# A two-layer encoder trunk: the MLP's up projection with two matmuls per weight tile instead of three, pinned transposes and a second priority level

## The chip, the cores and the metric

The kernel runs on one core of one Trainium2 chip. The metric is the device time of one execution in microseconds (us), taken as the median over runs. Five engines work side by side, each in the order of its own queue: TensorE (PE in the profile, with its weight loads as PEld), VectorE (DVE), ScalarE (ACT), GpSimd (POOL) and SyncE (SP), which issues most of the DMAs. They meet through semaphores only.

## The reference

Two layers over x of 256 tokens x 1024 channels, all in float32:

```python
for l in range(DEPTH):                                   # DEPTH = 2
    xn = rms_norm(x, norm_mix_g[l])
    x = x + mixer(xn, w_in[l], ...)                      # four branches, gates, w_out
    hn = rms_norm(x, norm_ffn_g[l])
    x = x + jnp.square(jax.nn.relu(hn @ w_ffn_up[l])) @ w_ffn_down[l]
return rms_norm(x, final_norm_g)

def mixer(xn, ...):
    h = xn @ w_in                                        # 1024 x 6176
    # split into glu, gq, gk, gv, gr, glr, aq, ak, av, pin, gate
    ys = jnp.stack([conv(..), gla(..), attention(..), pool(..)], axis=2)
    proj = jnp.einsum('btnc,ncd->btnd', ys, w_branch)    # 4 x (256 -> 1024)
    merged = jnp.sum(jax.nn.sigmoid(gate) * proj, axis=2)
    return merged @ w_out
```

The MLP is 1024 -> 4096 -> 1024. GLA is a chunked gated linear attention in both directions, attention is windowed, and the convolution has 31 taps.

## The kernel before

**Precision.** Every large product is made of float32r matmuls on split operands: a number is held as a high part (rounded to float32r) and a low part (the rest). A product is high x high + high x low + low x high, all summed in one PSUM region. `mm3` (lines 308 to 315) does that with the weights stationary and 256 tokens moving, `mm3t` (lines 317 to 324) with 128 tokens of x stationary and 512 weight columns moving.

**Weights.** `layer_loads` lists the weight pieces (128 partitions x 1024 numbers) in the order of their use. `fetch` (line 263) issues a piece's DMA on SP's queue into one of 3 raw buffers; `split_w` (line 271) makes the high part on ACT (line 278) and the low part on DVE (line 279), into 5 buffers of each kind. `piece` asks for a piece and lets `look_ahead` split four pieces ahead of it.

**Stages of a layer.** The gla, glu, qk, attention, pool and gate columns of w_in; the branches, with GLA and attention written as generators that the string `TURNS` (line 34) steps through in turn, one `next` per letter; the branch projections (`project`) and gates in the order `GATE_SEQ` (lines 40 to 46), where A, B, C, L stand for pool, attention, GLA and convolution; the transposes of the merged result (`turn_merged`); the output projection (`out_part`); the MLP (`up`, `down`) in 16 chunks of 256 hidden columns.

**The MLP.** `up(c)` makes one PSUM tile of a chunk: 8 row tiles k of 128 times 2 halves t of the 256 columns times `mm3`, 48 matmuls. Its eviction (lines 1150 to 1153) is a Relu on ACT, the square on DVE, the high part `hh` on ACT and the low part `hl` on DVE. `down(c)` is 24 matmuls of 512 columns into four accumulators that live for the whole MLP. The loop is up(2), down(1), up(3), down(2) and so on; on entry up(0) and up(1) are done in two halves of K, with `turn_x` between.

**Transposes.** x and the merged result lie with tokens on partitions for the sums and with channels on partitions for the matmuls. `turn` makes four 128 x 128 transposes on PE into one PSUM bank. `turn_x(xh, xl, h, g, behind)` turns the half h of x's channels and splits it (`split_x`, lines 427 to 434: high on ACT at line 430, low on DVE at line 431). `TokenStats.add` sums the squares of x for the norm (ACT, line 387); the norm's factor is applied at the end of the MLP, through `R2`.

**What sets the order.** The program is written with tiles; a planner orders each engine's queue by priority and by its own reckoning of when an instruction is ready, and puts in the semaphores. The priority is the place in the program; `urgent()` brings a block forward by 4000 places. `tc.issue_after(ins)` queues what a block writes for `ins`'s engine behind `ins` on that engine's queue, and adds no wait. PSUM has two pools of four banks, `ps_mm` (tag mm) and `ps_ax` (tag ax).

Of the kernel before, what the change touches and what calls it, by code (L numbers as in the profile page):

```python
# [33 lines left out]
TURNS = "agagagagggagggaggg"  # L34
# [138 lines left out]
def trunk_kernel(ctx: ExitStack, tc: tile.TileContext, x, w, prm, wup, poolw, cst, out, depth, dbg=None):  # L173
# [33 lines left out]

    def urgent():
        return tc.high_priority(offset=URGENT)

# [707 lines left out]
    for l in range(depth):  # L918
        if l == 0:
# [4 lines left out]
            for f in range(4):  # L924
# [3 lines left out]
                for t in (2 * f, 2 * f + 1):  # L928
                    split_x(xh, xl, t, xT[:, t, :], gain0)
# [122 lines left out]

        def project(n, h):
            first = n == BR_ORDER[0]
            wt = piece(l, ("br", n, h))
            for it in range(2):
# [5 lines left out]
                with urgent():  # L1062
# [6 lines left out]

        def turn_merged(h):  # L1070
            for f in (2 * h, 2 * h + 1):
                with urgent():
                    ps = turn(merged, f, mmt)
                    last_cast[:] = [S.copy(mh[:, 2 * f : 2 * f + 2, :], ps)]
                    V.tensor_tensor(
                        ml[:, 2 * f : 2 * f + 2, :], ps, mh[:, 2 * f : 2 * f + 2, :].bitcast(F32), ALU.subtract
                    )

        ENDS = {("gate", C, 1): ({1: conv},)}
        for what, n, h in GATE_SEQ:  # L1080
# [12 lines left out]
        fh = xs_p.tile([P, KD, T], F32R, tag="xs", name=nm("fh"))  # L1093
# [239 lines left out]
```

## Time and profile before

| | |
|---|---|
| median of 3 runs | 804.95 us (804.7 to 805.72) |
| the profiled execution, own time | 803.58 us |
| its span (first to last instruction of the program) | 801.6 us |
| PE busy | 782.3 us, 98%, 4810 matmuls |
| PEld busy (weight loads) | 687.9 us, 86%, 4810 loads |
| DVE busy | 558.4 us, 70%, 799 instructions |
| ACT busy | 473.5 us, 59%, 708 instructions |
| POOL busy | 10.6 us, 1% |
| read from HBM | 136.71 MB, 172 GB/s over the span |

The profile is of one execution. Matmuls are pipelined: the printed duration of one reaches past the start of the next, so what a matmul costs in a stream is the distance from its start to the next one's. The time in brackets behind an instruction is how long its engine stood idle before it, and the instruction that released it. A name such as mm or ax is a PSUM tile's tag, fh and fl are the high and low halves of x in the MLP, hi and lo those of the weights.

### The profile page before, as it was taken

To read this page: it belongs to the slowest core of one execution; us is meant where nothing else is said; L and a number is where in the kernel's file an instruction comes from. 1 tells how busy PE (TensorE), PEld (TensorE's weight loads), DVE (VectorE), ACT (ScalarE), POOL (GpSimd) and SP (SyncE) were. 2 spreads that over 40 slices of the span, in tenths; PEclk is the share of its full clock that TensorE was granted. 3 is DMA by queue.
4 is the path that set the end of the run, shared out by engine and by line. 5 is a ranking of instruction groups with operands and counts; after the bars stand their busy time and mean duration, and the time that the engine had idled before them with its cause. 6 is when DMAs were issued, how large, how long until landed. Compare 5 with 4: busy or idle time off the path is not lost.

```text
span 801.6 us, 12340 instructions
## 1 busy us (share of the span) xinstructions
PE 782.3 (98%) x4810; PEld 687.9 (86%) x4810; DVE 558.4 (70%) x799; ACT 473.5 (59%) x708; POOL 10.6 (1%) x22
## 2 busy tenths in 40 slices
PE   8999999999999999999999999999998999999996
PEld 8998887787798999999899987878788999999995
DVE  6789998887655555555577999878876655555553
ACT  6789795764654444444468787848545544444442
POOL 2000000000000000000000000000000000000000
PEclk9999999999999999999999999999999999999999
DMA  7755544465546555566455565435654565556631
GB/s 273 233 167 180 160 153 137 133 184 182 189 142 195 185 186 187 188 194 191 138 183 183 163 203 158 136 108 163 211 177 154 169 204 184 185 189 183 194 116 53
DMA packets 41130, 138.56 MB, mean 173 GB/s; under 512 B 4528, under 2 KB 7280, under 8 KB 41072
## 3 DMA queue, kind: packets, MB, share of 16 engines
q1 hardware_dynamic: 39616, 137.05, 54.0%
q10 hardware_dynamic: 1456, 0.73, 0.3%
q8 instruction: 37, 0.61, 0.3%
q14 instruction: 21, 0.17, 0.1%
HBM read 136.71 MB, written 1.05 MB: 172 GB/s over the span
## 4 chain that ended last, share of the span: by engine, by line
PE 91%; DVE 3%; DMA 3%; ACT 2%; issue 1%; ACTq 0%; DVEq 0%
PE mm L322 10%; PE mm L323 10%; PE mm L324 10%; PE mm L314 9%; PE mm L315 9%; PE mm L313 9%; PE ax L322 9%; PE ax L323 9%; PE ax L324 9%; DMA raw<-in_w_dram 2%; DVE lo L279 2%; ACT hi L278 1%; PE ax L657 1%; PE ax L836 1%; PE mm L1214 1%
## 5 line engine op out<-in xcount | busy, mean ns | idle before, releaser
L279 DVE TENSOR_TENSOR lo<-raw,hi 128x1024 fp32r<-128x1024 f32 (+2 forms) x260 | 313.9, 1208 | 202.4 <-ACT hi L278 193.0
L278 ACT CAST hi<-raw 128x1024 fp32r<-128x1024 f32 (+2 forms) x260 | 269.6, 1037 | 265.5 <-PE mm L314 113.9
L314 PE MATMUL mm<-fl,hi 128*128 128x256 f32 x512 | 144.6, 284 | 3.0 <-DVE fl L431 3.0
L313 PE MATMUL mm<-fh,hi 128*128 128x256 f32 x512 | 143.6, 283 | 1.4 <-ACT fh L430 1.4
L315 PE MATMUL mm<-fh,lo 128*128 128x256 f32 x512 | 144.2, 283 | 0.0
L322 PE MATMUL mm<-hi,xh 128*128 128x512 f32 (+1 forms) x320 | 122.6, 387 | 1.4 <-ACT xh L430 1.2
L323 PE MATMUL mm<-lo,xh 128*128 128x512 f32 (+1 forms) x320 | 122.5, 383 | 0.4 <-DVE lo L279 0.4
L324 PE MATMUL mm<-hi,xl 128*128 128x512 f32 (+1 forms) x320 | 121.1, 382 | 0.0
L314 PEld LDWEIGHTS mm<-fl,hi 128*128 128x128 f32 x512 | 98.0, 192 | 4.8 <-DVE fl L431 3.8
L313 PEld LDWEIGHTS mm<-fh,hi 128*128 128x128 f32 x512 | 97.5, 192 | 2.9 <-ACT fh L430 1.8
L322 PE MATMUL ax<-hi,hh 128*128 128x512 f32 x256 | 100.0, 390 | 0.0
L323 PE MATMUL ax<-lo,hh 128*128 128x512 f32 x256 | 100.0, 390 | 0.0
L315 PEld LDWEIGHTS mm<-fh,lo 128*128 128x128 f32 x512 | 98.0, 192 | 0.1
L324 PE MATMUL ax<-hi,hl 128*128 128x512 f32 x256 | 97.0, 389 | 0.0
L322 PEld LDWEIGHTS mm<-hi,xh 128*128 128x128 f32 x320 | 59.8, 188 | 14.1 <-ACT xh L430 1.5
L323 PEld LDWEIGHTS mm<-lo,xh 128*128 128x128 f32 x320 | 60.1, 188 | 12.4 <-issue 1.0
L324 PEld LDWEIGHTS mm<-hi,xl 128*128 128x128 f32 x320 | 60.0, 188 | 11.3 <-issue 0.2
L324 PEld LDWEIGHTS ax<-hi,hl 128*128 128x128 f32 x256 | 48.1, 188 | 10.2
L322 PEld LDWEIGHTS ax<-hi,hh 128*128 128x128 f32 x256 | 48.2, 188 | 9.2
L323 PEld LDWEIGHTS ax<-lo,hh 128*128 128x128 f32 x256 | 48.2, 188 | 9.0
L315 PE MATMUL mm<-xh,lo 128*128 128x256 f32 x160 | 45.4, 285 | 0.9 <-DVE lo L279 0.9
L314 PE MATMUL mm<-xl,hi 128*128 128x256 f32 x160 | 45.2, 283 | 0.0
(265 smaller groups left out, 1022.4 us busy)
## 6 DMA issues: line engine op xcount, KB each, us to landing
raw<-in_w_dram SPq DMA_DIRECT2D x252, 512.0 KB, 3.6
raw<-in_w_dram SPq DMA_DIRECT2D x6, 288.0 KB, 2.9
xT<-in_x_dram SPq DMA_DIRECT2D x4, 256.0 KB, 4.7
cst_t<-in_cst_dram SPq DMA_DIRECT2D x1, 608.0 KB, 5.6
out_dram<-yo SPq DMA_DIRECT2D x2, 256.0 KB, 2.4
out_dram<-yo ACTq DMA_DIRECT2D x2, 256.0 KB, 2.4
raw<-in_w_dram SPq DMA_DIRECT2D x1, 432.0 KB, 4.7
poolw_t<-in_poolw_dram SPq DMA_DIRECT2D x2, 128.0 KB, 4.3
```

Source lines behind the costliest of these rows:

```text
L278: a = S.copy(h[:, :n], r[:, :n])
L279: V.tensor_tensor(lo[:, :n], r[:, :n], h[:, :n].bitcast(F32), ALU.subtract)
L313: mm(o, a, xh[:, kx, :], start=start, stop=False, skip_group_check=True)
L314: mm(o, a, xl[:, kx, :], start=False, stop=False, skip_group_check=True)
L315: return mm(o, b, xh[:, kx, :], start=False, stop=stop, skip_group_check=True)
L322: mm(o, xh[:, kx, tk], wh[:, k, :], start=start, stop=False)
L323: mm(o, xh[:, kx, tk], wl[:, k, :], start=False, stop=False)
L324: return mm(o, xl[:, kx, tk], wh[:, k, :], start=False, stop=stop)
L657: mm(ot[:, h, :], pt[:, jt, h, it * P : (it + 1) * P], qkv[:, jt, 384 + 64 * g : 448 + 64 * g], start=jt == 0, stop=jt == 1,)
L836: mm(ps[32 * b : 32 * b + 32, jt], kk[:, j0 : j0 + 32], q[:, :, j0 : j0 + 32], start=True, stop=True, tile_position=(0, 32 * b),)
L1214: mm(ps[:, t, :], xt[:, it, c : c + P], dgs[it], start=True, stop=True)
```

## The change

Five things change together.

1. In `up`, the two halves of x lie side by side in a tile `fx` of [128, 4, 2, 256], so that one 512-column matmul takes a high weight tile to both: high x high lands in the first half of a PSUM bank, high x low in the second. The low weight tile meets the high half in a 256-column matmul onto the first half. Each of the two 128-column halves of a chunk now has a bank of its own, so a chunk holds two of the four banks of `ps_mm`. At eviction ACT copies the second half to SBUF, DVE adds it to the first, and the square takes the sum; the Relu on ACT is gone.
2. `turn_x` returns its last transpose, and the next group of matmuls (`out_part(3,1)`, `up(1)`'s first half, `down(15)` of the second half, the second `gvl`) is queued behind it. `turn_merged(0)` moves from behind ("br", C, 1) to behind the first half of ("br", L, 1).
3. A second level of priority, `critical()`, of 8000 places, is used for the transposes and splits of x, the merged transposes, the last branch's merging, the additions to x and part of the tail.
4. The sums of squares for the MLP's norm move from the end of the output projection to behind the first chunks of the MLP, at plain priority, and `st.inverse()` with them.
5. `TURNS` is shorter: GLA takes nine steps instead of twelve, so that its tail runs where `next(turns["g"], None)` stands behind ("br", B, 0), and attention's last two steps come earlier.

```diff
-TURNS = "agagagagggagggaggg"
+TURNS = "agagagaggagggag"
...
+    def after(t):
+
+        return tc.issue_after(t.ins) if t is not None else nullcontext()
+
     def urgent():
         return tc.high_priority(offset=URGENT)
+
+    def critical():
+        return tc.high_priority(offset=2 * URGENT)
 
     URGENT = 4000
...
-    def split_x(xh, xl, kt, src, g):
-
-        with urgent():
-            a = S.activation(xh[:, kt, :], src, AF.Copy, scale=g[:, kt : kt + 1])
-            V.scalar_tensor_tensor(
-                xl[:, kt, :], src, g[:, kt : kt + 1], xh[:, kt, :].bitcast(F32), ALU.mult, ALU.subtract
-            )
+    def split_x(xh, xl, src, gain):
+
+        with critical():
+            a = S.activation(xh, src, AF.Copy, scale=gain)
+            V.scalar_tensor_tensor(xl, src, gain, xh.bitcast(F32), ALU.mult, ALU.subtract)
         return a
...
-                nc.tensor.transpose(ps[:, t, it * P : (it + 1) * P], src[:, it, c : c + P], ident)
-        return ps
-
-    def turn_x(xh, xl, h, g, behind):
+                last = nc.tensor.transpose(ps[:, t, it * P : (it + 1) * P], src[:, it, c : c + P], ident)
+        return ps, last
+
+    def turn_x(parts, h, g, behind):
 
         with tc.issue_after(behind.ins):
-            turn_x_now(xh, xl, h, g)
-
-    def turn_x_now(xh, xl, h, g):
-        for f in (2 * h, 2 * h + 1):
-            with urgent():
-                ps = turn(xt, f, axt)
-            for t in range(2):
-                split_x(xh, xl, 2 * f + t, ps[:, t, :], g)
+            for f in (2 * h, 2 * h + 1):
+                with critical():
+                    ps, last = turn(xt, f, axt)
+                for t in range(2):
+                    kt = 2 * f + t
+                    split_x(*parts(kt), ps[:, t, :], g[:, kt : kt + 1])
+        return last
...
         for i, (k0, k1) in cuts if l == 0 else cuts[:2]:
-            done = gvl(i, k0, k1)
+            with after(turned if l and i == 1 else None):
+                done = gvl(i, k0, k1)
             if l and i == 0:
-                turn_x(xh, xl, 1, col(l, 0, 8), done)
+                turned = turn_x(x_parts, 1, col(l, 0, 8), done)
...
                 th = gates.pop((n, h, it))
-                with urgent():
+                if (n, h, it) == (L, 1, 0):
+                    with tc.issue_after(done.ins):
+                        turn_merged(0)
+                with critical() if n == L else urgent():
...
-            if (what, n, h) == ("br", C, 1):
-                with tc.issue_after(done.ins):
-                    turn_merged(0)
...
-        fh = xs_p.tile([P, KD, T], F32R, tag="xs", name=nm("fh"))
-        fl = xs_p.tile([P, KD, T], F32R, tag="xs", name=nm("fl"))
+
+        fx = [xs_p.tile([P, KD // 2, 2, T], F32R, tag="xs", name=nm("fx")) for _ in range(2)]
+
+        def f_parts(kt):
+            a = fx[kt // 4][:, kt % 4]
+            return a[:, 0, :], a[:, 1, :]
+
...
+        turned = None
         for h in range(2):
             for i in (2, 3):
-                done = out_part(i, h)
+                with after(turned if (i, h) == (3, 1) else None):
+                    done = out_part(i, h)
                 if (i, h) == (2, 1):
-                    turn_x(fh, fl, 0, col(l, 8, 8), done)
+                    turned = turn_x(f_parts, 0, col(l, 8, 8), done)
             for it in range(2):
                 xv = xt[:, it, 512 * h : 512 * h + 512]
-                with urgent():
+                with critical():
                     V.scalar_tensor_tensor(xv, acc[it, h], 0.5, xv, ALU.mult, ALU.add)
-            for it in range(2):
-                with urgent():
-                    st.add(it, h)
...
             if c not in ups:
-                ups[c] = mmt()
+                ups[c] = [mmt((P, 2, T)) for _ in range(2)]
             ps = ups[c]
             for i in parts:
-                wt = piece(l, (("up", c), i))
+                wh, wl = piece(l, (("up", c), i))
                 for k in range(4):
+                    f = fx[i][:, k]
                     for t in range(2):
-                        kk = 4 * i + k
-                        done = mm3(ps[:, t, :], wt, k, t * P, fx, kk, kk == 0 and t == 0, kk == 7)
+                        w1 = slice(t * P, (t + 1) * P)
+                        first, last = i + k == 0, (i, k) == (1, 3)
+                        mm(ps[t], wh[:, k, w1], f, start=first, stop=False, skip_group_check=True)
+                        done = mm(
+                            ps[t][:, 0, :], wl[:, k, w1], f[:, 0, :], start=False, stop=last, skip_group_check=True
+                        )
...
             r = gh_p.tile([P, 2, T], F32, tag="gh", name=nm("r"))
+            z = t2()
...
             with urgent():
-                S.activation(r, ps, AF.Relu)
-                V.scalar_tensor_tensor(r, ps, 0.0, r, ALU.max, ALU.mult)
+                for t in range(2):
+                    S.copy(z[:, t, :], ps[t][:, 1, :])
+                    V.tensor_tensor(r[:, t, :], ps[t][:, 0, :], z[:, t, :], ALU.add)
+                V.scalar_tensor_tensor(r, r, 0.0, r, ALU.max, ALU.mult)
                 S.copy(hh, r)
                 V.tensor_tensor(hl, r, hh.bitcast(F32), ALU.subtract)
...
             for c in range(2):
-                done = up(c, (i,))
+                with after(turned if (i, c) == (0, 1) else None):
+                    done = up(c, (i,))
                 if (i, c) == (0, 0):
-                    turn_x(fh, fl, 1, col(l, 8, 8), done)
-        with urgent():
-            R2 = st.inverse()
+                    turned = turn_x(f_parts, 1, col(l, 8, 8), done)
+        for h in range(2):
+            for it in range(2):
+                st.add(it, h)
+        R2 = st.inverse()
...
             for h in range(2):
                 for c in (14, 15):
-                    done = down(c, (0, 1), (h,))
+                    with after(turned if (c, h) == (15, 1) else None):
+                        done = down(c, (0, 1), (h,))
                     if (c, h) == (14, 1):
-                        turn_x(xh, xl, 0, col(nxt, 0, 8), done)
+                        turned = turn_x(x_parts, 0, col(nxt, 0, 8), done)
...
                     add_mlp(it, h)
-                    with urgent():
+                    with critical():
                         st.add(it, h)
```

## Rows read from the trace of the kernel before

**Rows 1.** The page: engines' busy time, PE's granted clock by slice.

```profile
PE 782.3 (98%) x4810; PEld 687.9 (86%) x4810; DVE 558.4 (70%) x799; ACT 473.5 (59%) x708; POOL 10.6 (1%) x22
...
PEclk9999999999999999999999999999999999999999
```

**Rows 2.** The page: the chain that ended last, by engine.

```profile
PE 91%; DVE 3%; DMA 3%; ACT 2%; issue 1%; ACTq 0%; DVEq 0%
```

**Rows 3.** Order of time, PE, one MLP chunk: start, duration, line, operands, count.

```profile
249.18 0.28 PE L315 MATMUL mm<-fh,lo 128*128 128x256 f32 x1
249.29 0.28 PE L313 MATMUL mm<-fh,hi 128*128 128x256 f32 x1
...
254.69 0.40 PE L322 MATMUL ax<-hi,hh 128*128 128x512 f32 x1
254.93 0.40 PE L323 MATMUL ax<-lo,hh 128*128 128x512 f32 x1
...
256.08 0.39 PE L322 MATMUL ax<-hi,hh 128*128 128x512 f32 x1
...
259.93 0.39 PE L324 MATMUL ax<-hi,hl 128*128 128x512 f32 x1
```

**Rows 4.** Groups by line and form: count | busy us, mean ns | idle.

```profile
L279 DVE TENSOR_TENSOR lo<-raw,hi 128x1024 fp32r<-128x1024 f32 x252 | 307.8, 1223 | 199.8 <-ACT hi L278 190.7 <-issue 8.6
...
L1151 DVE SCALAR_TENSOR_TENSOR r<-mm,r 128x512 f32<-128x512 f32 x32 | 21.9, 684 | 1.6 <-ACT r L1150 1.6
...
L1150 ACT ACTIVATE r<-mm 128x512 f32<-128x512 f32 x32 | 18.9, 592 | 1.9 <-PE mm L315 1.9
...
L431 DVE SCALAR_TENSOR_TENSOR fl<-ax,prm_t,fh 128x256 fp32r<-128x256 f32 x16 | 7.1, 475 | 0.0
L430 ACT ACTIVATE fh<-ax,prm_t 128x256 fp32r<-128x256 f32 x16 | 6.7, 468 | 0.0
```

**Rows 5.** Windows, steady MLP: PE, PEld, DVE, ACT, POOL busy, clock, DMA.

```profile
232.00:400.00 168.00, 168.00 (x1059) 152.74 (x1058) 93.48 (x95) 79.07 (x94) 0.00 (x0) 1.00 0.58 183
```

**Rows 6.** Order of time, DVE, that chunk's last step of the eviction.

```profile
259.87 0.68 DVE L1153 TENSOR_TENSOR hl<-r,hh 128x512 fp32r<-128x512 f32 x1
```

**Rows 7.** Order of time, PE and DVE, entry to the first MLP.

```profile
216.07 1.04 PE L442 MATMUL ax<-cst_t,xt 128*128 128x128 f32 x8
...
216.36 1.28 DVE L1122 SCALAR_TENSOR_TENSOR xt<-ax,xt 128x512 f32<-128x512 f32 x2
...
217.79 0.39 PE L313 MATMUL mm<-fh,hi 128*128 128x256 f32 x1 [0.68 <-ACT fh L430]
...
219.22 0.38 PE L314 MATMUL mm<-fl,hi 128*128 128x256 f32 x1 [0.93 <-DVE fl L431]
...
226.64 0.39 PE L314 MATMUL mm<-fl,hi 128*128 128x256 f32 x1 [0.54 <-DVE fl L431]
```

**Rows 8.** Order of time, PE, behind the first merged transposes.

```profile
189.82 0.50 PE L322 MATMUL mm<-hi,ysh 128*128 128x512 f32 x1 [0.55 <-DVE gate L1066]
```

**Rows 9.** Order of time, PE, the first matmul of the second layer.

```profile
402.51 0.40 PE L322 MATMUL mm<-hi,xh 128*128 128x288 f32 x1 [1.23 <-ACT xh L430]
```

**Rows 10.** Order of time, PE and ACT, the end of GLA.

```profile
139.31 0.35 PE L895 MATMUL ax<-g,o64r 128*128 128x256 f32 x1 [0.86 <-ACT g L886]
...
139.67 1.28 ACT L888 ACT_TABLE_LOAD   x1
...
140.58 0.39 PE L896 MATMUL ax<-g,o64r 128*128 128x256 f32 x1 [0.92 <-DVE g L889]
...
141.60 0.50 PE L322 MATMUL mm<-hi,ysh 128*128 128x512 f32 x1 [0.40 <-ACT ysh L462]
...
529.56 0.50 PE L322 MATMUL mm<-hi,ysh 128*128 128x512 f32 x1 [0.67 <-ACT ysh L462]
```

**Rows 11.** Order of time, DVE, the tail.

```profile
793.23 0.42 DVE L1215 TENSOR_TENSOR yo<-mm,prm_t 128x256 f32<-128x256 f32 x1 [0.96 <-PE mm L1214]
793.68 0.22 DVE L1246 SCALAR_TENSOR_TENSOR re<-rt,ms 128x1 f32<-128x1 f32 x1
```

More of the change, by code (lines that the diff above doesn't have):

```diff
@@ L1 @@
-from contextlib import ExitStack
+from contextlib import ExitStack, nullcontext
 import numpy as np
@@ L928, in trunk_kernel @@
                 for t in (2 * f, 2 * f + 1):
-                    split_x(xh, xl, t, xT[:, t, :], gain0)
+                    split_x(xh[:, t, :], xl[:, t, :], xT[:, t, :], gain0[:, t : t + 1])
             state["raw"] = state["next"] = 4
@@ L1051, in gate, with turn_merged @@
                 gates[n, h, it] = th
+        def turn_merged(h):
+            for f in (2 * h, 2 * h + 1):
+                with critical():
+                    ps, _ = turn(merged, f, mmt)
+                    last_cast[:] = [S.copy(mh[:, 2 * f : 2 * f + 2, :], ps)]
+                    V.tensor_tensor(
+                        ml[:, 2 * f : 2 * f + 2, :], ps, mh[:, 2 * f : 2 * f + 2, :].bitcast(F32), ALU.subtract
+                    )
         def project(n, h):
@@ L1068, in project @@
             return done
-        def turn_merged(h):
-            for f in (2 * h, 2 * h + 1):
-                with urgent():
[L1073 to L1077, printed above, removed]
         ENDS = {("gate", C, 1): ({1: conv},)}
@@ L1113, in trunk_kernel @@
                     turn_merged(1)
+        turned = None
         for h in range(2):
             for i in (2, 3):
-                done = out_part(i, h)
+                with after(turned if (i, h) == (3, 1) else None):
+                    done = out_part(i, h)
                 if (i, h) == (2, 1):
-                    turn_x(fh, fl, 0, col(l, 8, 8), done)
+                    turned = turn_x(f_parts, 0, col(l, 8, 8), done)
             for it in range(2):
                 xv = xt[:, it, 512 * h : 512 * h + 512]
-                with urgent():
+                with critical():
                     V.scalar_tensor_tensor(xv, acc[it, h], 0.5, xv, ALU.mult, ALU.add)
-            for it in range(2):
-                with urgent():
-                    st.add(it, h)
         with tc.issue_after(last_cast[0].ins):
             S.preload_act_table_set(LN_EXP)
-        fx = (fh, fl)
         hid = {}
@@ L1135, in up @@
             if c not in ups:
-                ups[c] = mmt()
+                ups[c] = [mmt((P, 2, T)) for _ in range(2)]
             ps = ups[c]
             for i in parts:
-                wt = piece(l, (("up", c), i))
+                wh, wl = piece(l, (("up", c), i))
                 for k in range(4):
+                    f = fx[i][:, k]
                     for t in range(2):
-                        kk = 4 * i + k
-                        done = mm3(ps[:, t, :], wt, k, t * P, fx, kk, kk == 0 and t == 0, kk == 7)
+                        w1 = slice(t * P, (t + 1) * P)
[3 more added lines that the diff above has]
+                            ps[t][:, 0, :], wl[:, k, w1], f[:, 0, :], start=False, stop=last, skip_group_check=True
+                        )
             if 1 not in parts:
@@ L1184, in add_mlp @@
             xv = xt[:, it, 512 * h : 512 * h + 512]
-            with urgent():
+            with critical():
                 V.scalar_tensor_tensor(xv, acc2[it, h], R2[:, it : it + 1], xv, ALU.mult, ALU.add)
+        turned = None
         if nxt < depth:
@@ L1190, in trunk_kernel, with x_parts @@
             xl = xs_p.tile([P, KD, T], F32R, tag="xs", name=nm("xl"))
+            def x_parts(kt, xh=xh, xl=xl):
+                return xh[:, kt, :], xl[:, kt, :]
             for h in range(2):
                 for c in (14, 15):
-                    done = down(c, (0, 1), (h,))
+                    with after(turned if (c, h) == (15, 1) else None):
+                        done = down(c, (0, 1), (h,))
                     if (c, h) == (14, 1):
-                        turn_x(xh, xl, 0, col(nxt, 0, 8), done)
+                        turned = turn_x(x_parts, 0, col(nxt, 0, 8), done)
                 for it in range(2):
@@ L1231, in trunk_kernel @@
                     add_mlp(it, h)
-                    with urgent():
+                    with critical():
                         st.add(it, h)
@@ L1239, in trunk_kernel @@
                             V.scalar_tensor_tensor(ms, st.ss[:, it, 1:2], 1.0 / D, m0, ALU.mult, ALU.add)
-                with urgent():
+                with critical():
                     o = br.tile([P, 1], F32, tag="rt", name=nm("rt"), bufs=2)
```

## The prediction

> **What bounds the kernel now.** I read the page's busy table and clock line first: TensorE (PE) is busy 782.3 of 801.6 us, at a granted clock of 1.00 throughout, which is the 2.4 GHz level [rows 1]. The chain that ended last agrees: 91% of it is PE [rows 2]. So the end moves only if PE gets fewer or shorter matmuls, or waits less. For the matmuls I read PE's order of time in one chunk of the MLP [rows 3]. From 249.18 to 254.69 us 46 matmuls of 256 columns start: 5.51/46 = 0.120 us each. The last 17 steps of the 512-column ones, 256.08 to 259.93, take 3.85/17 = 0.2265 us each. At 2.4 GHz the columns alone are 0.1067 and 0.2133 us, so both widths carry about 13 ns on top per matmul. That fixed part is the price that the change attacks. The printed durations (0.28 and 0.39) overlap and are no cost.
>
> For the waits I read the idle time in brackets. PE stands still for long at few places only: on entering each MLP [rows 7], at the merged transposes [rows 8], between the layers [rows 9], around the end of the GLA branch [rows 10] and in the tail. A matmul after such a wait also prints about 0.1 us more than its usual duration (0.39 for 0.28 in rows 7); I count that with the wait.
>
> **Up projection.** A weight tile met x in three 256-column matmuls; now it meets high and low halves in one of 512 and one of 256. Columns are the same 768, but one matmul and one weight load of three go. Per pair: before 3 x 0.120 = 0.360, after 0.2265 + 0.120 = 0.3465 us, so 13 ns less. There are 16 chunks x 8 row tiles x 2 halves x 2 layers = 512 of them: 512 x 0.0133 = 6.8 us; I take **6.7**. The trace has no stretch that alternates widths. Its switches bound it: the first gap after a switch to 256 is 0.11, the first after a switch to 512 is 0.24 [rows 3]. With 0.11 + 0.2265 the pair saves 0.0235 (12.0 us), with 0.24 + 0.12 it saves nothing. The steady values lie between and are what long runs show, so I keep them; bounds 0 to 12.0.
> The Trainium skill, "TensorE: Matmul & The Clock Gate", section "Back-to-back issue gap", gives an isolated warm matmul N/2.4 + 2.5 ns; by that this part would be an estimated 512 x 2.5 ns = 1.3 us. The trace speaks against it with its 13 ns at both widths [rows 3].
>
> **Eviction of a chunk.** One ScalarE (ACT) Relu of 512 goes; two ACT copies of 256, at 0.47 each as the x split, and two VectorE (DVE) adds, at 0.475 as the split's low part, come [rows 4]. DVE does its 0.68 us square as before, now from SBUF. Per chunk ACT gains about 0.94 - 0.59 = 0.35 us and DVE 0.95 us. In the steady MLP they are busy 79 and 93 of 168 us, 15 periods of 11.2 (48 x 0.12 + 24 x 0.2265) [rows 5]: 5.3 and 6.2 per chunk, to become 5.6 and 7.2 of 11.0. Neither binds. The delay: today the chain runs from the up projection's last matmul, just ahead of 254.69 [rows 3], to the end of hl at 259.87 + 0.68 = 260.55 [rows 6], 5.9 us. I add 0.9 of work on the way and up to two hops behind a 1.22 us weight split [rows 4], so 9.2 at most. The low projection of that chunk comes one down and one up later, 24 x 0.2265 + 16 x 0.3465 = 5.44 + 5.54 = 11.0 us. Cost **0**, with 1.8 us to spare; if the cover went, every chunk would pay (rival 3).
>
> **First chunk of an MLP.** A chunk now takes two PSUM banks instead of one, and the pool has four. Chunks 0 and 1 fill it, so chunk 2 can't run ahead until chunk 0 is evicted. PE's cover is the second half of chunk 1, 8 x 0.3465 = 2.77 us. Freeing the banks needs about 0.2 + 0.47 + 0.47 + 0.47 = 1.6 us, 2.8 behind one split; the high half of the hidden tile needs 1.6 + 0.68 + 0.6 (as the Relu) = 2.9 [rows 4], or 4.2. So a new wait of 0 to 1.6 us per layer; I take **-0.5 each, -1.0**, near the lower end, as either chunk 2 or the down projection may go first. Queued behind it is everything on PE.
>
> **Entry to the MLP.** Before, the eight transposes of x's first half stand behind the last out-projection matmul (216.07), and PE waits for their split: 0.68 for fh, 0.93 for fl, later 0.54 for the second half; with restarts 0.79 + 1.03 + 0.65 = 2.47 us [rows 7], and the same three in layer 1. After, they are queued before the last out part, 12 x 0.2265 = 2.72 us earlier; x's first half can be added as soon as out_part(3,0) is done, again 2.72 us ahead, and takes 1.28 for its two adds [rows 7]. Four ACT and four DVE splits, 4 x 0.47 = 1.9 us each way [rows 4], fit into the cover, and their higher priority lets at most one weight split ahead. The second half is queued behind up(0, first half): its x adds take the same 1.28 us, PE has 2.77. Queued behind these transposes are out_part(3,1) and up(1); they wait only if the x adds come later than that. Nothing else takes the waits' place, so **4.9** for both layers; bounds 0 to 4.9. The four Squares of a layer leave this place for a stretch where ACT is half idle. No moved step issues a DMA; SP's loads wait for the splits, which run four pieces (about 11 us) ahead, and POOL is not passed.
>
> **Merged transposes.** They move behind six more matmuls (1.36 us) with their DVE work ahead of the splits. The wait for a bank, 0.55 + 0.11 = 0.66 per layer [rows 8], should go, but the turn and the second half of the projection now need four banks in a row: 0 to 1.3 gained, or up to 1.4 lost (a split ahead, 1.22, less some cover); I take **1.0**.
>
> **Between the layers.** PE waits 1.23 + 0.11 = 1.34 for xh [rows 9]. The first half is covered as above. The second is queued behind only six 288-column matmuls (0.8 us), while its add ends about 1.0 us after the down projection: a new wait of 0.3, behind it gvl(1). **1.0**, bounds -0.2 (one split ahead) to 1.3.
>
> **GLA.** Nine steps instead of twelve: the tail is queued behind ("br", B, 0), and attention's last step comes before GLA's ninth. In layer 0 PE waits three times, 0.86, 0.92 and 0.40, with restarts 2.47 us; the last is for ysh, which stands on ACT behind a 1.28 us table load [rows 10]. With the tail out of PE's way the first two go, and ysh ahead of the Squares takes most of the third: 2.0, bounds 0 (if ysh stays behind the table load, PE waits at the same place) to 2.5. Layer 1 has 0.78 at ysh [rows 10]: 0.4, bounds 0 to 0.8. Sum **2.4**. The tail's result is needed two gates later, 2 x 48 x 0.2265 = 22 us, so its lateness is covered.
>
> **Tail.** The second half's scale starts at 793.68 on DVE, right behind the first half's output multiply of 793.23 [rows 11]; with priority it may go ahead and gain up to 0.8, or come no sooner because ACT hands over late: **0.3**, bounds 0 to 0.8.
>
> **Rivals.** 1. *Only the matmuls count*: the pins trade waits, for PE now stops at a transpose instead of behind it, and two banks per chunk add theirs. The clean cover of rows 7 speaks against, the untested orders of ACT and DVE for. Gain 6.7: 804.95 - 6.7 = 798.2, or down to nothing if new waits eat it. 2. *The 13 ns don't go with a matmul*: alternating widths pay the slow switch each time, 0.24 + 0.12, and the first term is 0: 15.3 - 6.7 = 8.6, 796.4. The steady 0.12 and 0.2265 speak against it. By the skill's 2.5 ns, above, 1.3 of it would stay, 795.0. 3. *Slower*: the longer eviction misses the down projection in every chunk. It decides once the chain exceeds 11.0 us (now 5.9, reckoned 9.2); at 12.0 some 14 chunks x 2 layers wait 1.0 each, 28 - 15.3 = 12.7 lost, 817.7. Break-even is a chain of 11.55. DVE and ACT half idle in rows 5 speak against.
>
> **How the numbers follow.** 6.7 - 1.0 + 4.9 + 1.0 + 1.0 + 2.4 + 0.3 = 15.3 us. The profiled execution took 803.58, of which 801.6 is span: 786.3 span, 788.3 in all. The median of the runs is 1.37 higher; I apply the sum to it: 804.95 - 15.3 = 789.65, say 789.7. Chances: forecast (784 to 794) 0.66, rival 1 0.16, rival 2 0.08, rival 3 0.06, a gain beyond the forecast (the 12.0 bound) 0.04. Range 784 to 800: it takes in rivals 1 and 2 but for the worst of rival 1. What a measurement of this kernel can tell from no change is about 0.2%, 1.6 us. Slower by more is rival 3, 0.06; within it the worst of rival 1, 0.04; faster 0.90.
>
> **What would show it.** 512 matmuls and weight loads fewer, and a chunk's period of 10.98 instead of 11.2: right on the first term; 11.2 or more: rival 2 or 3. In the order of time: eight transposes of x between two out parts with no wait behind, then a first down projection with a wait under 1.6. No wait at L895's successors before ("br", B, 0). A regular wait before each down projection for hh or hl would make rival 3 true.

## The result, and the profile after

The changed kernel takes 791.67 us, median of 4 runs (791.41 to 792.47). Before it was 804.96 (804.7 to 805.72), so the ratio is 0.9835, 95% interval 0.9818 to 0.9852: 13.3 us less. The forecast was 789.7 in a range of 784 to 800. The sign, the range and the size are right, but several terms of the sum are not, and they partly cancel.

The page of the changed kernel, as [rows 1, 2] of before: engines' busy time, PE's granted clock by slice, the chain that ended last by engine.

```profile
PE 778.6 (99%) x4298; PEld 659.6 (84%) x4298; DVE 585.3 (74%) x863; ACT 476.1 (60%) x740; POOL 9.6 (1%) x22
...
PEclk9999999999999999999999999999999999999999
...
PE 96%; DVE 1%; DMA 1%; ACT 1%; issue 1%; DVEq 0%
```

PE has 4810 - 4298 = 512 matmuls and as many weight loads fewer, as reckoned. Its share of the chain rose from 91% to 96%: what DVE, DMA and ACT held before is mostly gone. The profiled execution has a span of 789.6 us (791.41 in all) against 801.6 (803.58): 12.0 us of span. The medians differ by 13.3, and about 1.3 of it lies outside the two traces and goes with the clock (at which place, no trace shows): of 43 other executions of before on record, the ten with a granted clock of 1.000, like the profiled one, took 803.45 to 803.96 us and the 33 with 0.993 to 0.998 took 804.37 to 807.55, while all four of the changed kernel have 0.999 or 1.000.

Order of time on PE in the MLP of the changed kernel (start, duration, line, operands, count), at the place that answers to [rows 3], a chunk's last up matmuls and the first down matmul:

```profile
249.05 0.40 PE L1153 MATMUL mm<-fx,hi 128*128 128x512 f32 x1
249.29 0.28 PE L1154 MATMUL mm<-fx,lo 128*128 128x256 f32 x1
249.40 0.40 PE L329 MATMUL ax<-hi,hh 128*128 128x512 f32 x1
```

Start to start it is 0.24 after a 512-column matmul and 0.11 after a 256-column one; a whole chunk's 16 pairs, from 254.87 to 260.51, take 5.64 us, 0.353 per pair. Before it was 3 x 0.120 = 0.360; the forecast said 0.3465. So a pair saves 7 ns and not 13.5, and 512 pairs save 3.6 us instead of 6.7. Down projections start at 249.40 and 260.51, a period of 11.11 us, between the 11.2 of before and the 10.98 foretold.

The eviction of the chunk that ends at 249.40, on ACT and DVE in order of time; [rows 6] showed its last step before:

```profile
249.25 0.37 ACT L1165 COPY t<-mm 128x256 f32<-128x256 f32 x1 [1.50 <-PE mm L1154]
249.66 0.42 DVE L1166 TENSOR_TENSOR r<-mm,t 128x256 f32<-128x256 f32 x1 [0.65 <-ACT t L1165]
...
252.21 0.69 DVE L1167 SCALAR_TENSOR_TENSOR r<-r 128x512 f32<-128x512 f32 x1
253.31 0.61 ACT L1168 CAST hh<-r 128x512 fp32r<-128x512 f32 x1
254.58 0.69 DVE L1169 TENSOR_TENSOR hl<-r,hh 128x512 fp32r<-128x512 f32 x1
```

From the last up matmul (starting at 249.29) to the end of hl at 255.27 it is about 6 us: hardly longer than the 5.9 of before, and far from the 11.0 at which every chunk would wait. Rival 3 is out for the steady part.

Entry to the first MLP on PE, against [rows 7]:

```profile
211.27 1.03 PE L447 MATMUL ax<-cst_t,xt 128*128 128x128 f32 x8
212.06 0.47 PE L329 MATMUL ax<-hi,mh 128*128 128x512 f32 x1
...
214.91 0.39 PE L1153 MATMUL mm<-fx,hi 128*128 128x512 f32 x1
...
217.79 1.04 PE L447 MATMUL ax<-cst_t,xt 128*128 128x128 f32 x8
218.59 0.47 PE L1153 MATMUL mm<-fx,hi 128*128 128x512 f32 x1
```

No bracket of idle time stands anywhere: both groups of transposes have work behind them, and by the time the up projection starts its operands are ready. The three waits of [rows 7] are gone in both layers. Between the layers, against [rows 9], a wait stands at another place:

```profile
390.64 0.39 PE L331 MATMUL ax<-hi,hl 128*128 128x512 f32 x1
391.42 0.33 PE L447 MATMUL ax<-cst_t,xt 128*128 128x128 f32 x1 [0.39 <-DVE xt L1205]
392.08 0.98 PE L447 MATMUL ax<-cst_t,xt 128*128 128x128 f32 x7 [0.33 <-DVE xt L1205]
392.82 0.48 PE L329 MATMUL ax<-hi,hh 128*128 128x512 f32 x1
```

It is at the transposes themselves: 0.39 + 0.33 printed, 1.14 by start to start (against 1.44 before). At the merged transposes the wait of [rows 8] is gone, and the two steps of PE from 192.45 take 0.46 and 0.34 instead of 0.2265 (row below), so about half of it comes back. The tail's wait is as before: its second matmuls start after 0.86 of idle time in both kernels (row below; before at 794.95).

```profile
192.45 0.39 PE L330 MATMUL ax<-lo,mh 128*128 128x512 f32 x1
192.91 0.74 PE L331 MATMUL ax<-hi,ml 128*128 128x512 f32 x2
...
783.00 2.02 PE L1239 MATMUL mm<-t,xt 128*128 128x128 f32 x16 [0.86 <-DVE t L1274]
```

### The profile page after: what moved, and what is told of

The parts are those of the page before. It is cut to its first block, busy times and chain, and to the rows that moved or that the text cites. A ratio compares the mean times of both kernels' runs of the same rounds, so it can differ in the third digit from the quotient of the medians.

```text
span 789.6 us, 11416 instructions
## 1 busy us (share of the span) xinstructions
PE 778.6 (99%) x4298; PEld 659.6 (84%) x4298; DVE 585.3 (74%) x863; ACT 476.1 (60%) x740; POOL 9.6 (1%) x22
## 4 chain that ended last, share of the span: by engine, by line
PE 96%; DVE 1%; DMA 1%; ACT 1%; issue 1%; DVEq 0%
PE mm L1153 15%; PE mm L329 11%; PE mm L331 11%; PE mm L330 10%; PE ax L331 9%; PE ax L329 9%; PE ax L330 9%; PE mm L1154 8%; PE mm L322 2%; PE mm L321 2%; PE mm L320 2%; PE ax L840 1%; PE ax L661 1%; PE ax L447 1%; DMA raw<-in_w_dram 1%
## 5 line engine op out<-in xcount | busy, mean ns | idle before, releaser
L1153 PE MATMUL mm<-fx,hi 128*128 128x512 f32 x512 | 181.9, 398 | 0.0
L1154 PE MATMUL mm<-fx,lo 128*128 128x256 f32 x512 | 143.1, 281 | 0.0
L1153 PEld LDWEIGHTS mm<-fx,hi 128*128 128x128 f32 x512 | 96.0, 188 | 23.2 <-DVE fx L438 0.3
L1154 PEld LDWEIGHTS mm<-fx,lo 128*128 128x128 f32 x512 | 96.6, 189 | 1.7 <-DVE lo L286 0.3
L1165 ACT COPY t<-mm 128x256 f32<-128x256 f32 x64 | 23.4, 369 | 45.7 <-PE mm L1154 45.7
L320 PE MATMUL mm<-xh,hi 128*128 128x256 f32 x160 | 45.2, 284 | 0.0
```

What stands on the lines that cost most here:

```text
L320: mm(o, a, xh[:, kx, :], start=start, stop=False, skip_group_check=True)
L1153: mm(ps[t], wh[:, k, w1], f, start=first, stop=False, skip_group_check=True)
L1154: done = mm(ps[t][:, 0, :], wl[:, k, w1], f[:, 0, :], start=False, stop=last, skip_group_check=True)
L1165: S.copy(z[:, t, :], ps[t][:, 1, :])
```

## The experiments

Two accounts of the 13.3 us were to be told apart. **Theory:** each part gives its own term, the matmuls some 3.6 us, the pins and the priority the entry, the shorter GLA its 2.4, and the 7 ns lost per pair are the price of changing the width twice. **Rivals:** the matmul form, the pins and the place of the Squares work only together; the second priority level is idle; the 7 ns have nothing to do with the order. In the table, "before" is the kernel before on the same chip, and the ratio is to it.

| kernel | median us | before | ratio, 95% interval | span |
|---|---|---|---|---|
| changed kernel | 791.67 | 804.96 | 0.9835 (0.9818 to 0.9852) | 789.6 |
| up alone | 804.56 | 804.90 | 1.0001 (0.9991 to 1.0011) | 801.6 |
| old up | 800.40 | 804.90 | 0.9948 (0.9936 to 0.9960) | 798.6 |
| old up, late Squares | 795.24 | 804.75 | 0.9883 (0.9869 to 0.9896) | 793.6 |
| grouped by piece | 791.21 | 804.90 | 0.9831 (0.9819 to 0.9844) | 789.5 |
| grouped from chunk 2 | 789.50 | 804.75 | 0.9811 (0.9797 to 0.9824) | 787.1 |
| no pins | 802.11 | 805.70 | 0.9951 (0.9936 to 0.9967) | 800.3 |
| old Squares | 799.59 | 805.70 | 0.9923 (0.9908 to 0.9938) | 797.5 |
| one priority | 791.50 | 805.70 | 0.9827 (0.9811 to 0.9843) | 790.1 |
| old turns | 794.07 | 805.70 | 0.9856 (0.9841 to 0.9872) | 792.2 |
| turn later | 791.24 | 804.90 | 0.9834 (0.9821 to 0.9846) | 789.3 |
| grouped from 2, turn later | 788.43 | 804.75 | 0.9798 (0.9785 to 0.9811) | 787.0 |
| longer eviction | 807.10 | 804.75 | 1.0031 (1.0022 to 1.0040) | 806.2 |

**1. Up alone.** The kernel before with the new matmuls, banks and eviction, and nothing else.

```diff
-                ups[c] = mmt()
+                ups[c] = [mmt((P, 2, T)) for _ in range(2)]
...
+                        mm(ps[t], wh[:, k, w1], f, start=first, stop=False, skip_group_check=True)
+                        done = mm(
+                            ps[t][:, 0, :], wl[:, k, w1], f[:, 0, :], start=False, stop=last, skip_group_check=True
+                        )
```

> The kernel before with the up projection's new matmuls, the two banks and the new eviction alone; order, priorities and TURNS as before. Theory: in the changed kernel a 512-column matmul between two of 256 takes 0.236 us and the 256 behind it 0.117, 0.353 a pair where three of 256 took 0.360; so this part alone is worth 512 x 0.007 = 3.6 us: 804.96 - 3.6 = 801.4. Rival 1, the steady prices of the prediction (0.3465): 6.7, 798.2. Rival 2, two banks per chunk take away PE's run-ahead on entering the MLP while the waits there are still in place: 1 to 3 us of the gain go, 802.4 to 804.4.

It gained nothing, though its steady pairs take the same 0.353 us. Its entry to the MLP, on PE:

```profile
219.50 0.50 PE L1146 MATMUL mm<-fx,hi 128*128 128x512 f32 x1 [2.12 <-DVE fx L431]
...
227.43 0.50 PE L1146 MATMUL mm<-fx,hi 128*128 128x512 f32 x1 [1.15 <-DVE fx L431]
...
229.35 0.50 PE L1146 MATMUL mm<-fx,hi 128*128 128x512 f32 x1 [0.24 <-DVE fx L431]
```

The first 512-column matmul needs the high and the low half at once. Before, the first matmul could start on the high half alone and the low one came later [rows 7]. Start to start, the three waits sum to 2.33 + 1.31 + 0.40 = 4.04 us per layer instead of 2.67: two layers lose 2.7 of the 3.6 us. The 0.9 that should be left is not seen; why stays open. The merged matmul makes the entry dearer, and that is a cost the prediction didn't have, since it costed the parts one by one.

**2. Old up, and old up with late Squares.** The changed kernel with the up projection and eviction of before; then the same with the Squares of the norm queued on ACT behind chunk 0's hh cast.

```diff
-                ups[c] = [mmt((P, 2, T)) for _ in range(2)]
+                ups[c] = mmt()
...
+        with tc.issue_after(first_hh[0].ins):
+            for h in range(2):
+                for it in range(2):
+                    st.add(it, h)
```

> The changed kernel with the up projection of before (three matmuls of 256 columns, one bank per chunk, Relu and square); pins, priorities and TURNS as changed. Theory: it loses the 3.6 us of the matmuls and keeps all else, 791.67 + 3.6 = 795.3. Rival, the prediction's price: 798.4. If more than half of the whole gain of 13.3 hung on the up projection, it would be above 798.4.

> The changed kernel with the up projection and its eviction of before (as in the run with the old up projection, 800.4 us), but with ScalarE's Squares of the norm queued behind the hh cast of hidden chunk 0, where the changed kernel ran them by itself. In the run with the old up projection these Squares stood on ScalarE ahead of the casts of the first half (211.62 to 212.85 us), and TensorE still waited 0.88 and 1.41 us in each layer. Theory (the entry waits come from the Squares' place on ScalarE, not from the three-matmul form): the waits go, 2 x 2.29 = 4.6 us less, 795.8 us (795 to 797). Rival (the three-matmul form itself meets a wait there, since its order needs the high half alone and then the low half): the waits stay and the time stays at 800.4 us.

The first missed: 800.4, because PE waits at the entry although the pins hold. PE and ACT of "old up":

```profile
217.17 0.39 PE L320 MATMUL mm<-fh,hi 128*128 128x256 f32 x1 [0.72 <-ACT fh L437]
218.71 0.38 PE L321 MATMUL mm<-fl,hi 128*128 128x256 f32 x1 [1.15 <-DVE fl L438]
...
211.62 0.62 ACT L394 ACTIVATE t<-xt 128x512 f32<-128x512 f32 x1
...
212.85 1.03 ACT L285 CAST hi<-raw 128x1024 fp32r<-128x1024 f32 x1
```

Two Squares and their sums stand on ACT from 211.62 to 212.85, ahead of the casts of the first half that PE is waiting for. In the changed kernel the same instructions run elsewhere, although the program text puts them at the same place and at plain priority:

```profile
227.79 0.64 ACT L394 ACTIVATE t<-xt 128x512 f32<-128x512 f32 x1
```

Why the scheduler moves them so far when only the up projection differs was not settled; I take it that the new ACT copy's tile comes ahead of theirs in the same pool. That their place is the cause of the waits is shown: queued late by hand, the waits are gone and the old up takes 795.24. What then remains between it and the changed kernel, 3.6 us by the medians (3.9 by the ratios), is the up projection's form alone: its matmuls, banks and eviction. It agrees with 512 x 7 ns. The Trainium skill, "TensorE: Matmul & The Clock Gate", section "Back-to-back issue gap", would make it 512 x 2.5 ns, an estimated 1.3 us; no run agrees with that.

**3. Grouped by piece, and from chunk 2.** Eight matmuls of 512 columns, then eight of 256, for each weight piece: two changes of width instead of sixteen. Then the same with pairs alternating in chunks 0 and 1.

```diff
+                for some in [kts] if c > 1 else [[kt] for kt in kts]:
+                    for kt in some:
+                        high(*kt)
+                    for kt in some:
+                        done = low(*kt)
```

> The changed kernel with a piece's eight 512-column matmuls first and its eight of 256 behind them; the same matmuls, so two switches of width per piece instead of sixteen. Theory, the 7 us that the first term lacks of its steady price sit at the switches: a piece takes about 8 x 0.227 + 8 x 0.120 = 2.78 us instead of 8 x 0.353 = 2.82, and with 64 pieces 2.7 us go: 789.0. Rival, a 512-column matmul on the split x is 9 ns slower wherever it stands: 791.7, no change.

> The changed kernel with the up matmuls of a weight piece grouped (eight of 512 columns, then eight of 256) for hidden chunks 2 to 15 only; chunks 0 and 1 keep the alternating pairs. Theory (each pair pays 7 ns for the two changes of width, and only the first two chunks lost in the run that grouped them all): 28 chunks x (5.64 - 5.56) = 2.2 us less, 789.4 us against the changed kernel's 791.7 and the grouped one's 791.2. Rival (the grouped order costs elsewhere as well, for example a wait for a PSUM bank in later chunks): no gain, 791.0 to 791.7 us.

One chunk's up projection in "grouped from chunk 2" (a line for each run of equal matmuls), and under it the first MLP chunks of "grouped by piece":

```profile
254.59 1.98 PE L1151 MATMUL mm<-fx,hi 128*128 128x512 f32 x8
256.40 1.12 PE L1155 MATMUL mm<-fx,lo 128*128 128x256 f32 x8
257.36 2.00 PE L1151 MATMUL mm<-fx,hi 128*128 128x512 f32 x8
259.20 1.11 PE L1155 MATMUL mm<-fx,lo 128*128 128x256 f32 x8
260.15 0.40 PE L329 MATMUL ax<-hi,hh 128*128 128x512 f32 x1
```

```profile
228.33 0.97 PE L1150 MATMUL mm<-fx,hi 128*128 128x512 f32 x3 [0.41 <-DVE r L1170]
```

260.15 - 254.59 = 5.56 us for the chunk, where the alternating one takes 260.51 - 254.87 = 5.64 and the one before took 48 x 0.12 = 5.76. So grouped pairs cost 5.56/16 = 0.3475, close to the 0.3465 of the steady rows, and most of the 7 ns is what alternating the widths costs. With all chunks grouped, most of that gain is eaten at the entry: from the first up matmul to the first down one PE takes 18.7 us per layer instead of 17.9. Of this, 0.58 us (0.41 printed) is a wait for the PSUM bank of chunk 0, released by DVE's addition. That is the prediction's "first chunk" wait, at its size; the changed kernel happens not to have it. So the median falls by 0.5 instead of the 2.7 expected. With the first two chunks left alternating the gain is 2.2 us as expected.

**4. No pins, old Squares, one priority.** Each undoes one thing of the changed kernel: after() pins nothing; the Squares stand where they stood before, urgent; critical() is no higher than urgent().

```diff
-        return tc.issue_after(t.ins) if t is not None else nullcontext()
+        return nullcontext()
...
+            for it in range(2):
+                with urgent():
+                    st.add(it, h)
...
-        return tc.high_priority(offset=2 * URGENT)
+        return tc.high_priority(offset=URGENT)
```

> The changed kernel without the four pins behind the transposes of x (out_part(3, 1), up(1), down(15, 1) and the second gvl are free again); priorities, squares, TURNS and up projection as changed. Theory, the pins hold the place of the transposes: without them they go back behind the last out part, as before, and PE waits there for both halves of the split, 2.3 us a layer as in the kernel with the up projection alone, and the first two chunks' waits of 1.3 and 0.4: 791.67 + 2 x 3 = 797. Rival, the priority and the absent squares do the work and the planner puts the transposes early by itself: 791.7.

> The changed kernel with the sums of squares back at the end of the output projection at their old priority; pins, second priority level, TURNS and up projection as changed. In the kernel with the old up projection the entry waits (0.88 + 1.41 us a layer) stayed although the pins stood, and there the Squares ran on ACT ahead of the splits of x. Theory, it is the Squares' place that decides: two of 0.81 us go ahead of fh on ACT, and the waits at the MLP's first matmul come back, 2 to 3 us a layer: 791.67 + 4 to 6 = 795.7 to 797.7. Rival, the second priority level lets the splits of x go first wherever the Squares are: 791.7.

> The changed kernel with the second priority level made equal to the first; all else as changed. Theory, on entering the MLP a split of x then stands behind weight splits on ACT (1.05 us) and DVE (1.22 us) of equal priority; the cover of 2.7 us takes one but not two of them, so part of the entry waits comes back, 0.5 to 1.5 us a layer, and something of the merged wait (0.75 a layer): 791.67 + 2 to 4 = 793.7 to 795.7. Rival, the pins alone carry it: 791.7.

Without pins the entry is that of "up alone" (2.12 + 1.30 + 0.40 per layer, start to start), and the wait between the layers is the 1.44 of before. With the old Squares it is one wait per layer. Both cost more than was expected, and more than the waits themselves. PE in "old Squares", and windows of the same place (busy us of PE, PEld, DVE, ACT, POOL with counts, then PE's granted clock, DMA share and GB/s):

```profile
218.07 0.50 PE L1156 MATMUL mm<-fx,hi 128*128 128x512 f32 x1 [2.15 <-DVE fx L438]
```

```profile
218.00:219.00 1.00, 0.93 (x4) 0.79 (x5) 0.82 (x5) 0.07 (x1) 0.00 (x0) 0.73 0.29 82
219.00:220.00 1.00, 1.00 (x5) 0.90 (x4) 0.00 (x0) 0.00 (x0) 0.00 (x0) 0.50 0.86 324
...
222.00:223.00 1.00, 1.00 (x10) 0.96 (x9) 0.09 (x1) 1.00 (x2) 0.00 (x0) 1.00 0.00 0
```

After 2.15 us of standing still, PE's granted clock is 0.50 of full speed, the 1.2 GHz level, for some 3.4 us; start to start a pair then takes 0.64 us instead of 0.353. That loses about 1.7 us more, in both layers: 2 x (2.3 + 1.7) = 8.0, and the median is 7.9 above the changed kernel. Without pins the clock falls in the first layer only, in the profiled execution: 2 x (2.12 + 1.30 + 0.40) + 1.7 + 0.3 = 9.6 of the 10.4 by the medians (9.3 by the ratios). One priority costs nothing (0.9827 against 0.9835, the intervals overlap), with the pins in place: my theory was wrong, its rival right.

**5. Old turns.** The changed kernel with the old order of the GLA and attention steps.

```diff
-TURNS = "agagagaggagggag"
+TURNS = "agagagagggagggaggg"
```

> The changed kernel with the TURNS of before (GLA twelve steps, attention's last step behind GLA's ninth); all else as changed. Theory, the three waits around GLA's end come back in layer 0 (2.8 us start to start) and the one in layer 1 (0.9): 791.67 + 2.8 to 3.7 = 794.5 to 795.4. Rival, only layer 0's come back because layer 1's was removed by the priorities: 794.5; or none: 791.7.

```profile
138.96 0.35 PE L899 MATMUL ax<-g,o64r 128*128 128x256 f32 x1 [0.86 <-ACT g L890]
140.23 0.39 PE L900 MATMUL ax<-g,o64r 128*128 128x256 f32 x1 [0.92 <-DVE g L893]
...
141.25 0.69 PE L329 MATMUL mm<-hi,ysh 128*128 128x512 f32 x1 [0.40 <-ACT ysh L466]
...
145.00 0.39 PE L331 MATMUL mm<-hi,xl 128*128 128x512 f32 x1
```

All waits of [rows 10] are back, in layer 1 too (0.67 at 525.31), 3.65 us start to start. Yet the median rises by 2.4 only (the ratios say 1.7, the spans 2.6), less than the 2.8 to 3.7 expected. And part of the 2.6 is no wait: right behind the three waits of layer 0 PE's granted clock falls to 0.50 for some 3.4 us (window below). The nine steps of 512 columns from 141.25 to 145.00 take 3.75 us, where nine at 0.228 would take 2.05; less the usual restart, some 1.6 us go to the clock.

```profile
142.00:143.00 1.00, 1.00 (x3) 0.73 (x3) 0.52 (x1) 0.45 (x1) 0.00 (x0) 0.50 0.38 152
```

So the new order removes 3.65 of waiting and spends more than half of it again. Part of where is seen in sums of PE's start-to-start times: the 192 small matmuls of L840 take 8.3 us with the new turns and 6.5 with the old ones. By layer, from the first branch projection to the first matmul on the merged result, PE takes 96.2 us with the old turns and 93.2 with the new ones in layer 0, but 94.1 and 94.3 in layer 1. Without the clock the new order is thus worth some 1.4 us in layer 0 and nothing in layer 1.

**6. Turn later, and with the grouping.** The next layer's first-half transposes go behind the first k step of the last chunk's second half.

```diff
+                    if (c, h) == (15, 1):
+                        done = down(c, (0, 1), (h,), (0,))
+                        turned = turn_x(x_parts, 0, col(nxt, 0, 8), done)
+                        with after(turned):
+                            done = down(c, (0, 1), (h,), (1,))
```

> The changed kernel with the transposes of the next layer's first half queued behind the first half of K of down(15, 1) instead of behind down(14, 1), and the second half of K behind them. Theory, in the changed kernel the planner has put down(14, 1) ahead of down(15, 0), so these transposes stand right behind the matmuls whose sums they need and wait 0.55 + 0.59 us for the adds to x; six matmuls (1.36 us) between cover the adds: 791.67 - 1.0 = 790.7. Rival, the six matmuls left behind the transposes are too few for the splits of xh and xl and the wait comes back at the second layer's first matmul: 791.7 or above.

> The kernel with grouped matmuls from chunk 2 on, and with the next layer's first-half transposes put behind the first k step of the last chunk's second half. The trace of that move alone showed the wait between the layers go from 1.14 to 0.48 us, which its median did not resolve. Theory: 0.6 us below the kernel with the grouping alone, 788.8 us (788.2 to 789.4). Rival (the move is worth nothing in the median): the same time as with the grouping alone.

The wait falls, though not by the 1.0 expected; shown here for the combined kernel:

```profile
391.35 0.27 PE L447 MATMUL ax<-cst_t,xt 128*128 128x128 f32 x1
391.90 0.76 PE L447 MATMUL ax<-cst_t,xt 128*128 128x128 f32 x5 [0.28 <-DVE xt L1213]
```

1.14 became 0.48 us start to start. Alone it can't be seen in the median (791.24 against 791.67, overlapping ranges). With the grouping the median is 1.1 us below the grouping alone, and their runs don't overlap (788.07 to 788.76, 788.87 to 789.62), though the intervals of the ratios do and the two spans are equal but for 0.1. (The profiled execution with the move reached its first branch projection 0.4 us later, 98.06 against 97.70, in a stretch that the move doesn't touch.) I count 0.7 as shown by the trace and the rest as open. This kernel, 788.43 us, beats both: 2% under the kernel before.

**7. Longer eviction.** Four more ACT passes over r in each chunk's eviction, in place.

```diff
+                for _ in range(4):
+                    S.copy(r, r)
                 S.copy(hh, r)
```

> The changed kernel with four more ScalarE passes over r (each 128 x 512, in place, values unchanged) in the eviction of each hidden chunk, between the squaring and the hh cast. It makes the chain from a chunk's last up matmul to its hl 4 x about 0.63 = 2.5 us longer, from about 6.2 to 8.7 us, and ScalarE busier by 32 x 2.5 = 80 us. Theory (the eviction is covered, the chain has until about 11.0 us): no change, 791.7 us within 0.8 us, and no new wait ahead of a down matmul in the steady part; only the last chunk of each layer, whose down matmuls follow its own eviction more closely, may show one. Rival (the cover is nearly used up, the reckoning of 11.0 us is wrong or ScalarE's queue decides): TensorE waits in each chunk, 32 x up to 2.5 us, up to 870 us.

PE at the first down projection of the first layer and at the last chunk's, then windows of the half clock behind the first and of twelve steady chunks:

```profile
237.23 0.80 PE L329 MATMUL ax<-hi,hh 128*128 128x512 f32 x1 [3.96 <-ACT hh L1170]
...
396.34 0.50 PE L329 MATMUL ax<-hi,hh 128*128 128x512 f32 x1 [2.40 <-ACT hh L1170]
```

```profile
238.00:239.00 1.00, 1.00 (x4) 0.81 (x3) 0.97 (x3) 0.00 (x0) 0.00 (x0) 0.50 0.66 188
...
257.00:390.00 133.00, 133.00 (x674) 112.72 (x673) 82.77 (x97) 90.96 (x132) 0.00 (x0) 1.00 0.59 186
```

Both sides were half right. In the steady chunks 2.5 us more of eviction cost nothing: PE is busy 133.00 of 133.00. But the kernel is 15.4 us slower than the changed one, all of it at the edges: 4.13 us of waiting at each MLP's first down projection and 2.56 at the first layer's last chunk, 10.8 in all start to start, and the rest mostly in stretches at half clock behind them. In the changed kernel the eviction of chunk 0 starts at 226.04 (rows below) and its down projection at 232.78: 6.7 us, where a steady chunk has 11.3 (249.25 to 260.51). Its hh is ready 0.7 us before it is needed. DVE has squared r by 229.68, but the cast of hh stands on ACT behind two of the Squares that change 4 moved there (230.23 to 231.38). With the four passes hh is ready 5.1 us later (237.18) and not 2.5, since weight splits and copies of other chunks run between them on ACT.

```profile
226.04 0.37 ACT L1165 COPY t<-mm 128x256 f32<-128x256 f32 x1 [3.41 <-PE mm L1154]
...
231.47 0.61 ACT L1168 CAST hh<-r 128x512 fp32r<-128x512 f32 x1
```

## Why the prediction held, step by step

- **What bounds the kernel**: right. PE's share of the chain rose to 96%, and each gain is a matmul fewer or a wait fewer on PE.
- **Up projection, 6.7**: mis-sized; 3.6 by trace and by the old up with late Squares. The step that failed is "The steady values lie between and are what long runs show, so I keep them". The kernel alternates widths at every matmul, so no steady value applies. The prediction had read the gaps after a switch, 0.11 and 0.24, and put them together both ways as bounds; the pattern is the sum of just these two, 0.24 + 0.11 to 0.12. Rival 2 had a true core, half of the term.
- **Eviction, 0**: right for the steady chunks: the chain is 6 us, less than the 9.2 reckoned. But the cover of 11.0 was taken for every chunk; at the first one hh has 0.7 us to spare, and the last one is short as well, which the longer eviction shows. There it was luck that the added work didn't reach PE.
- **First chunk, -1.0**: no such wait in the changed kernel. It is real as soon as the order changes (0.58 per layer when grouped by piece).
- **Entry, 4.9**: the gain came in full; the waits sum to 5.3 us start to start. The reasons given, an earlier place in the queue and a higher priority, were incomplete. The pins carry it, the priority does nothing where they stand, and the Squares' place, which the prediction mentioned as a side effect ("leave this place for a stretch where ACT is half idle"), is as necessary as the pins. Without the pins, or with early Squares (put there by hand, or by the scheduler when the old up is back), PE waits again.
- **Merged transposes, 1.0**: 1.5 of wait gone, about 0.7 back at the two steps from 192.45 in each layer's copy of this place, so 0.8.
- **Between the layers, 1.0**: failed, 0.3. The prediction covered the first half "as above" and looked for the new wait at the second. But all three other groups of the last two chunks' down projection ran first, and the last matmuls ahead of the transposes were those whose sums they need: the additions to x (DVE L1205, from 390.62) start just at the last one.
- **GLA, 2.4**: mis-sized. The waits went in full, 3.65 where the term had 2.4 for them, but the prediction put the cost of the new order at nothing, and that order spends over 2 us again. From the first branch projection to the first matmul on the merged result (rows below) PE took 95.39 us before and 93.20 after in layer 0; in layer 1, 94.89 and 94.27. Of these 2.8 us, 1.5 are the merged wait, so 1.3 are left. That the old turns' median lies 2.4 above, the very size of the term, is luck: their trace lost 1.6 to the clock, which the prediction didn't reckon with.

```profile
97.97 0.39 PE L322 MATMUL mm<-hi,ysh 128*128 128x512 f32 x1
193.36 0.39 PE L322 MATMUL ax<-hi,mh 128*128 128x512 f32 x1
```

```profile
97.66 0.39 PE L329 MATMUL mm<-hi,ysh 128*128 128x512 f32 x1
190.86 0.39 PE L329 MATMUL ax<-hi,mh 128*128 128x512 f32 x1
```

- **Tail, 0.3**: nothing; the second scale does start sooner behind the first multiply, 0.34 instead of 0.45 us, but PE's wait is 0.86 as before.

The sum by the profile is 3.6 + 0 + 5.3 + 0.8 + 0.3 + 1.3 + 0 = 11.3, against a span difference of 12.0; of the rest, 0.3 lies ahead of the first branch projection (97.97 and 97.66), and 0.4 stays open. The forecast of 15.3 was too high by 5.4 in the up, merged, boundary, GLA and tail terms and too low by 1.4 in the first chunk and the entry. That the medians differ by 13.3, nearer to it, is owed to 1.3 us that go with the clock, which no term had. Rival 1 is out: the matmuls are the smaller part of the gain.

The sum of the parts undone one by one is far above the whole: 9 for the old up, 9 to 10 for the pins, 7 to 8 for the Squares, some 2 for the turns, 28 us against 13. And up alone gains nothing. The parts don't add: each one of three brings back waits at the same boundary.

## What to carry to other kernels

Cost a matmul by the pattern in which it will be issued: rows of steady runs price grouped matmuls, and the gaps at a change of width price alternating ones; where pairs alternate, group them, except where the order of banks or operands at an edge forbids it. Reckon the cover of a chain at the first and the last pass of a loop separately from the steady ones. And when several edits guard the same boundary, don't hand out the gain among them: each may be needed for all of it, and one may be idle.

## What the runs showed of the hardware that was not expected

- Alternating 512 and 256 columns costs 0.353 us per pair, grouped eight by eight 0.3475; changing the width twice costs some 5 to 7 ns.
- A wait on PE can cost more than its length. After 2.15 us of idle time ("old Squares", both layers) the granted clock stood at 0.50 for some 3.4 us. After 1.92 us "no pins" lost clock in the first layer and not in the second, and after 2.12 us "up alone" lost it in neither (row below: the window behind its wait). Shorter waits can do it too: behind 0.86, 0.92 and 0.40 us in a row "old turns" lost it, while in the trace of before the same three [rows 10], and those of up to 0.93 us at the entry [rows 7], left the clock at 1.00. What decides it stays open.

```profile
220.00:221.00 1.00, 1.00 (x7) 0.86 (x7) 0.94 (x4) 0.34 (x1) 0.00 (x0) 1.00 0.80 254
```
